# A row softmax on one core: load 5 in two transfers of 14 and 2 rows, and store 0 issued after the 14 rows

## The chip, the core and the metric

The kernel runs on one core of a Trainium2 chip. The core has five engines with instruction streams of their own: TensorE (PE, not used here), VectorE (DVE), ScalarE (ACT), GpSimd (POOL) and SyncE (SP), which here issues all transfers. Sixteen DMA engines move data between the chip's memory (HBM) and the core's on-chip memory (SBUF, 128 partitions). The metric is device time in microseconds (us) of one execution; lower is better.

## The reference

A softmax over the last axis of a float32 array of 16 x 1024 x 512, that is, over 16,384 rows of 512 numbers:

```python
def reference(x):
    x_max = np.max(x, axis=-1, keepdims=True)
    exp_x = np.exp(x - x_max)
    return (exp_x / np.sum(exp_x, axis=-1, keepdims=True)).astype(np.float32)
```

Each of input and output is 33.55 MB, so 67.1 MB cross between HBM and SBUF at least once.

## The kernel before

**Tiles.** The rows are cut into 8 chunks of 2,048 rows. In a chunk each of the 128 partitions holds 16 rows, which lie one behind the other in HBM: 16 x 512 x 4 bytes = 32 KB per partition, 4 MB per chunk. The buffer `held` has 6 places of one chunk. Chunks 6 and 7 use the places of chunks 0 and 1 again, once these are stored. All work is done in place: `held` is loaded, turned into exponentials, scaled and stored.

**Groups.** Work on the engines goes by groups of 8 rows per partition, two groups per chunk, 16 in all (128 x 4,096 numbers each). For each group:

- DVE takes the negated maximum of each row (`rowmax`, L133);
- ACT takes exp(x - max) row by row, with the row's sum as a by-product (`exps`, L165, 8 instructions per group);
- DVE takes the reciprocal of the sums (L142);
- POOL multiplies the rows by it (`scale`, L144). For groups 12 to 15 DVE does this itself (`ON_VECTOR`).

DVE's order is written out: the maximum of group g, then the reciprocal (and for the last four, the product) of group g - 1.

**Transfers.** All 16 transfers go through one DMA queue that SP feeds. `ORDER` sets the order in which SP issues them: loads 0 to 5, stores 0, 1 and 2, loads 6 and 7, stores 3 to 7. Loads 0 to 5 are issued at once, the first ahead of the kernel's opening barrier (`loads_at_the_head`, with `AT_HEAD`). A store waits until both groups of its chunk are scaled (semaphore `scaled[k]`). Load 6 waits until store 0 has landed (`stored[0]`), load 7 until store 1 has. DVE's first maximum in a chunk waits until its load has landed (`loaded[k]`). SP works through its list in order: what stands behind a waiting instruction waits too. A transfer of one chunk is 128 pieces of 32 KB, 8 for each of the 16 DMA engines. At the end SP waits until the last stores have landed.

Of the kernel before, what the change touches and what calls it, by code (L numbers as in the profile page):

```python
# [1 line left out]

# [4 lines left out]

F32 = mybir.dt.float32
EXP = mybir.ActivationFunctionType.Exp
AX = mybir.AxisListType.X  # L10

CHUNK = 16
CHUNKS = 8
PLACES = 6
GROUP = 8
PER = CHUNK // GROUP
GROUPS = CHUNKS * PER
RING = PLACES * PER  # L20


ORDER = [("L", k) for k in range(PLACES)] + [
    ("S", 0),
    ("S", 1),
    ("S", 2),
    ("L", 6),
    ("L", 7),
    ("S", 3),
    ("S", 4),  # L30
    ("S", 5),
    ("S", 6),
    ("S", 7),
]


ON_VECTOR = (12, 13, 14, 15)


AT_HEAD = {mybir.EngineType.SP: 1}  # L40

def loads_at_the_head(nc):

    main, body = nc.main_func.blocks[0], nc.main_func.blocks[1]
    for engine, count in AT_HEAD.items():
        loads = [
            i
            for i in body.instructions  # L50
            if i.engine == engine and type(i).__name__ == "InstDMACopy"
        ][:count]
        barrier = next(
            n
            for n, i in enumerate(main.instructions)
            if i.engine == engine and type(i).__name__ == "InstDrain"
        )
        for load in loads:
            body.instructions.remove(load)
        main.instructions[barrier:barrier] = loads  # L60


@with_exitstack
def kernel(
    ctx: ExitStack,
    tc: tile.TileContext,
    x: bass.AP,
    out: bass.AP,
):
    nc = tc.nc  # L70
    nc.at_finalize(loads_at_the_head)
    P = nc.NUM_PARTITIONS

    x_rows = x.flatten_outer_dims().rearrange("(c p r) d -> c p r d", p=P, r=CHUNK)
    out_rows = out.flatten_outer_dims().rearrange("(c p r) d -> c p r d", p=P, r=CHUNK)
    n, _, _, d = x_rows.shape
    assert n == CHUNKS

    held = nc.alloc_sbuf_tensor("held", [P, PLACES * CHUNK, d], F32).ap()
    shift = nc.alloc_sbuf_tensor("shift", [P, GROUPS * GROUP], F32).ap()  # L80
    sums = nc.alloc_sbuf_tensor("sums", [P, GROUPS * GROUP], F32).ap()
    recip = nc.alloc_sbuf_tensor("recip", [P, GROUPS * GROUP], F32).ap()

    loaded = [nc.alloc_semaphore(f"loaded{k}") for k in range(CHUNKS)]
    stored = [nc.alloc_semaphore(f"stored{k}") for k in range(CHUNKS)]
    maxed = nc.alloc_semaphore("maxed")
    expd = nc.alloc_semaphore("expd")
    to_pool = nc.alloc_semaphore("to_pool")
    to_vector = nc.alloc_semaphore("to_vector")
    scaled = [nc.alloc_semaphore(f"scaled{k}") for k in range(CHUNKS)]  # L90

    def take(engine, semaphore, n):

        engine.wait_ge(semaphore, n).then_inc(semaphore, -n)  # L94

    def place(k):
        at = (k % PLACES) * CHUNK
        return held[:, at : at + CHUNK, :]

    def rows(g):  # L100
        at = (g % RING) * GROUP
        return held[:, at : at + GROUP, :]

    def stats(t, g):
        return t[:, g * GROUP : (g + 1) * GROUP]

    with tc.manual_schedule():  # L110
        for _, k in ORDER[:PLACES]:
            first = nc.sync.dma_start(out=place(k), in_=x_rows[k])
            first.then_inc(loaded[k], 16)
            tc.no_tile_sem_insts.add(first.ins.name)
    tc.close()
    tc.compile()  # L116

    reused = set()
    for what, k in ORDER[PLACES:]:
        if what == "L":  # L120
            if k >= PLACES:
                take(nc.sync, stored[k - PLACES], 16)
                reused.add(k - PLACES)
            nc.sync.dma_start(out=place(k), in_=x_rows[k]).then_inc(loaded[k], 16)
        else:
            take(nc.sync, scaled[k], PER)
            nc.sync.dma_start(out=out_rows[k], in_=place(k)).then_inc(stored[k], 16)


    def rowmax(g):  # L130
        if g % PER == 0:
            take(nc.vector, loaded[g // PER], 16)
        nc.vector.reduce_max(  # L133
            out=stats(shift, g), in_=rows(g), axis=AX, negate=True
        ).then_inc(maxed, 1)

    def scale(g):
        engine, ready = (
            (nc.vector, to_vector) if g in ON_VECTOR else (nc.gpsimd, to_pool)
        )  # L140
        take(nc.vector, expd, 1)
        nc.vector.reciprocal(out=stats(recip, g), in_=stats(sums, g)).then_inc(ready, 1)  # L142
        take(engine, ready, 1)
        engine.tensor_mul(  # L144
            out=rows(g),
            in0=rows(g),
            in1=stats(recip, g).unsqueeze(2).to_broadcast([P, GROUP, d]),
        ).then_inc(scaled[g // PER], 1)

    for g in range(GROUPS):  # L150
        rowmax(g)
        if g:
            scale(g - 1)
    scale(GROUPS - 1)


    nc.scalar.preload_act_table(EXP)  # L157

    def exps(first, turns):
        with nc.scalar.Fori(0, turns) as i:  # L160
            take(nc.scalar, maxed, 1)
            for r in range(GROUP):
                row = held[:, bass.ds(i * GROUP + r, 1), :]
                at = bass.ds(i * GROUP + (first * GROUP + r), 1)
                act = nc.scalar.activation(  # L165
                    out=row,
                    in_=row,
                    func=EXP,
                    bias=shift[:, at],
                    scale=1.0,  # L170
                    accum_out=sums[:, at],
                )
            act.then_inc(expd, 1)

    exps(0, RING)
    exps(RING, GROUPS - RING)


    for k in range(CHUNKS):
        if k not in reused:  # L180
            take(nc.sync, stored[k], 16)


# [1 line left out]
_INS = ['x']  # L185
_OUTS = [((16, 1024, 512), 'float32')]


# [23 lines left out]
```

## Time and profile before

| What | Value |
|---|---|
| Median of three runs | 160.18 us (160.12 to 160.20) |
| The profiled execution's own time | 160.32 us |
| Its span, first to last instruction | 159.0 us |
| HBM read and written | 33.55 and 33.55 MB, 422 GB/s over the span |
| Maxima on DVE (L133), 16 | 70.3 us busy, 4.398 us each |
| Exponentials on ACT (L165), 128 | 90.3 us busy, 0.706 us each |
| Products on POOL (L144), 12 | 83.8 us busy, 7.018 us each |
| Products on DVE (L144), 4 | 18.3 us busy, 4.576 us each |
| Issue of loads 0 to 5 by SP | from 0.00 to 3.23 us |
| Issue of stores 0, 1, 2 by SP | at 37.65, 51.60 and 65.55 us |
| Issue of loads 6, 7 by SP | at 71.28 and 81.05 us |
| Issue of the last store by SP | at 141.02 us |

The profile is of one execution with the hardware profiler on, which is why its own time stands beside the median. The span leaves out what lies before the first and after the last instruction. Busy times are per engine and overlap. A DMA issue on SP is short; the transfer itself goes on in the DMA engines, and "landing" is the moment at which its semaphore has counted all 16 engines. The profile also holds packet records: start, duration and size of each piece that a DMA engine moved.

### The profile page before, as it was taken

To read this page: it belongs to the slowest core of one execution; us is meant where nothing else is said; L and a number is where in the kernel's file an instruction comes from. 1 tells how busy PE (TensorE), PEld (TensorE's weight loads), DVE (VectorE), ACT (ScalarE), POOL (GpSimd) and SP (SyncE) were. 2 spreads that over 40 slices of the span, in tenths; PEclk is the share of its full clock that TensorE was granted. 3 is DMA by queue.
4 is the path that set the end of the run, shared out by engine and by line. 5 is a ranking of instruction groups with operands and counts; after the bars stand their busy time and mean duration, and the time that the engine had idled before them with its cause. 6 is when DMAs were issued, how large, how long until landed. Compare 5 with 4: busy or idle time off the path is not lost. (4 is left out here: it accounts for less than half of the span.)

```text
span 159.0 us, 740 instructions
## 1 busy us (share of the span) xinstructions
DVE 90.6 (57%) x36; ACT 92.0 (58%) x257; POOL 84.0 (53%) x16
## 2 busy tenths in 40 slices
DVE  0008959777977977887700000695999998740000
ACT  0300699999999999999993000059934929200000
POOL 0000009999999999999999999259200000000000
DMA  7999999999999999999999999999999999999995
GB/s 264 470 445 404 404 478 437 396 470 445 404 404 470 445 396 396 396 412 470 437 396 445 470 404 404 478 437 398 437 437 437 412 462 414 437 437 429 429 429 256
DMA packets 2306, 67.13 MB, mean 422 GB/s; under 512 B 256, under 2 KB 256, under 8 KB 256
## 3 DMA queue, kind: packets, MB, share of 16 engines
q1 hardware_dynamic: 2304, 67.11, 98.8%
q14 instruction: 2, 0.02, 0.0%
HBM read 33.55 MB, written 33.55 MB: 422 GB/s over the span
## 5 line engine op out<-in xcount | busy, mean ns | idle before, releaser
L165 ACT ACTIVATE held<-held,shift x128 | 90.3, 706 | 40.0 <-ACTq L94 40.0
L144 POOL TENSOR_TENSOR held<-held,recip 128x4096 f32<-128x4096 f32 x12 | 83.8, 7018 | 28.1 <-POOLq L94 28.1
L133 DVE TENSOR_REDUCE shift<-held 128x8 f32<-128x4096 f32 x16 | 70.3, 4398 | 33.3 <-DVEq L94 33.3
L165 ACT ACTIVATION_READ_ACCUMULATOR held<-held,shift x128 | 23.8, 186 | 0.0
L144 DVE TENSOR_TENSOR held<-held,recip 128x4096 f32<-128x4096 f32 x4 | 18.3, 4576 | 0.6
L142 DVE RECIPROCAL recip<-sums 128x8 f32<-128x8 f32 x16 | 3.2, 201 | 16.4 <-DVEq L94 16.4
L157 ACT ACT_TABLE_LOAD x1 | 1.3, 1283 | 4.0 <-PEq L116 4.0
L196 POOL MEMSET const-float32-0.0<- 128x1 f32 x1 | 0.1, 99 | 0.2 <-issue 0.2
L196 POOL MEMSET const-uint8-127<- 128x1 uint8 x1 | 0.1, 103 | 0.0
L196 POOL MEMSET const-bfloat16-1.0<- 128x1 bf16 x1 | 0.1, 102 | 0.0
L196 POOL MEMSET const-float32-1.0<- 128x1 f32 x1 | 0.1, 99 | 0.0
## 6 DMA issues: line engine op xcount, KB each, us to landing
held<-in_x_dram SPq DMA_DIRECT2D x8, 4096.0 KB, 29.9
out_dram<-held SPq DMA_DIRECT2D x8, 4096.0 KB, 28.3
```

Of the source, the lines that this page charges most:

```text
L133: nc.vector.reduce_max(out=stats(shift, g), in_=rows(g), axis=AX, negate=True).then_inc(maxed, 1)
L142: nc.vector.reciprocal(out=stats(recip, g), in_=stats(sums, g)).then_inc(ready, 1)
L144: engine.tensor_mul(out=rows(g), in0=rows(g), in1=stats(recip, g).unsqueeze(2).to_broadcast([P, GROUP, d]),).then_inc(scaled[g // PER], 1)
L157: nc.scalar.preload_act_table(EXP)
L165: act = nc.scalar.activation(out=row, in_=row, func=EXP, bias=shift[:, at], scale=1.0, accum_out=sums[:, at],)
L196: nc = _bacc.Bacc("TRN2", target_bir_lowering=False, num_devices=1)
```

## The change

Load 5 (rows 80 to 95 of each partition) becomes two transfers: rows 80 to 93 (28 KB per partition) and rows 94 and 95 (4 KB per partition). Both are issued at the head with the other loads. Behind them SP's list has a new entry "W": SP waits until the 14 rows have landed, then raises a new semaphore, `passed`, and only then comes to store 0. DVE's first maximum that needs these rows waits for `passed`, and for the landing of the 2 rows too. (SP's wait leaves `loaded` of the 14 rows as it is; it is taken back at the end.)

The diff also rewrites how chunks and DVE's order are written down: chunks are named by their first and last row, and DVE's order is a list (`M` maximum, `P` product on POOL, `V` product on DVE). The order of DVE, ACT and POOL that comes out is the same as before, as are all other transfers and the place of each in HBM and SBUF.

```diff
-ORDER = [("L", k) for k in range(PLACES)] + [
-    ("S", 0),
-    ("S", 1),
-    ("S", 2),
-    ("L", 6),
...
+BLOCKS = [(0, 16), (16, 32), (32, 48), (48, 64), (64, 80), (80, 96), (96, 112), (112, 128)]
+ORDER = [
+    ("L", (0, 16)),
...
+    ("L", (64, 80)),
+    ("L", (80, 94)),
+    ("L", (94, 96)),
+    ("W", (80, 94)),
+    ("S", (0, 16)),
+    ("S", (16, 32)),
+    ("S", (32, 48)),
+    ("L", (96, 112)),
+    ("L", (112, 128)),
+    ("S", (48, 64)),
...
+    ("S", (112, 128)),
 ]
+AHEAD = 7
...
+    def in_dram(rows, a, b):
+
+        first, last = next(k for k in BLOCKS if k[0] <= a and b <= k[1])
+        block = rows[first * P : last * P].rearrange("(p r) d -> p r d", p=P)
+        return block[:, a - first : b - first, :]
...
+    def load(k):
+        copy = nc.sync.dma_start(out=rows(*k), in_=in_dram(x_rows, *k))
+        copy.then_inc(loaded[k], 16)
+        return copy
...
+    for what, k in ORDER[AHEAD:]:
+        if what == "W":
+
+            nc.sync.wait_ge(loaded[k], 16).then_inc(passed, 1)
+        elif what == "L":
+            for s in stores:
+                if meets(s, k[0] - RING, k[1] - RING) and s not in taken:
+                    take(nc.sync, stored[s], 16)
+                    taken.add(s)
+            load(k)
         else:
-            take(nc.sync, scaled[k], PER)
-            nc.sync.dma_start(out=out_rows[k], in_=place(k)).then_inc(stored[k], 16)
...
     def rowmax(g):
-        if g % PER == 0:
-            take(nc.vector, loaded[g // PER], 16)
+        for k in loads:
+            if meets(k, *group(g)) and k not in seen:
+                if ("W", k) in ORDER:
+                    take(nc.vector, passed, 1)
+                else:
+                    take(nc.vector, loaded[k], 16)
+                seen.add(k)
...
+    for what, k in ORDER:
+        if what == "W":
+            take(nc.sync, loaded[k], 16)
```

## The prediction, made before the changed kernel was run

> **What bounds the kernel now.** I read the page first: the busy shares, the 40 slices, the DMA part and the chain that ended last.
>
> ```profile
> span 159.0 us, 740 instructions
> DVE 90.6 (57%) x36; ACT 92.0 (58%) x257; POOL 84.0 (53%) x16
> DMA  7999999999999999999999999999999999999995
> q1 hardware_dynamic: 2304, 67.11, 98.8%
> DVE held L144 3%
> ```
>
> No compute engine is busy for even 60% of the span, while the 16 DMA engines work in every slice and the one queue fills 98.8% of their time. The chain is nearly empty (3%): the last instruction waited for a transfer, and a transfer is no step of the chain. So the bound is the queue of sixteen 4 MB transfers, and a change is worth only what it does to a hole in that queue. To find holes I cut the span at the landings of successive transfers (issue start plus time to landing) and asked for the work in each stretch. The columns are start:end and length in us, the busy time of DVE, ACT and POOL with counts, the clock, the DMA share and GB/s.
>
> ```profile
> 0.00:12.34 12.34, 0.00 (x0) 1.28 (x1) 0.21 (x4) 1.00 0.93 382
> 12.34:22.03 9.69, 8.74 (x2) 4.82 (x13) 0.00 (x0) 1.00 1.00 433
> 41.45:51.16 9.71, 7.62 (x3) 9.71 (x29) 9.71 (x2) 1.00 1.00 432
> 51.16:61.44 10.28, 8.97 (x4) 10.28 (x30) 10.28 (x3) 1.00 1.03 408
> 61.44:71.20 9.76, 7.52 (x5) 9.76 (x29) 9.76 (x2) 1.00 1.00 430
> 80.97:90.78 9.81, 0.00 (x0) 4.06 (x12) 9.81 (x2) 1.00 0.99 428
> 90.78:100.47 9.69, 0.00 (x0) 0.00 (x0) 9.54 (x2) 1.00 1.00 433
> 100.47:110.33 9.86, 8.81 (x3) 5.00 (x15) 5.02 (x1) 1.00 1.02 435
> 110.33:120.08 9.75, 8.70 (x3) 6.40 (x19) 2.00 (x1) 1.00 1.02 438
> ```
>
> These are loads 0, 1, 4, 5, store 0, store 2, loads 6 and 7, and store 3. The usual transfer takes 9.7 us. Two do not: load 0, which starts from an empty queue, and load 5, the last before the first store, which takes 10.28, so 10.28 - 9.71 = 0.57 us too long. The second change from loads to stores (load 7, then store 3) costs only 0.15, and that from store 2 to load 6 nothing.
>
> Then I looked closely at load 5's end. Each DMA engine moves one partition's 32 KB in 1.21 us, and the 16 start together, so a fine cut shows bursts of starts and pauses (GB/s is credited to a packet's start).
>
> ```profile
> 57.35:58.05 0.70, 0.70 (x1) 0.70 (x4) 0.70 (x1) 1.00 1.80 749
> 58.05:58.65 0.60, 0.60 (x1) 0.60 (x3) 0.60 (x2) 1.00 0.00 0
> 58.65:59.25 0.60, 0.60 (x1) 0.60 (x3) 0.60 (x1) 1.00 3.31 874
> 59.25:60.55 1.30, 1.30 (x1) 1.30 (x5) 1.30 (x1) 1.00 0.00 0
> 60.55:61.20 0.65, 0.65 (x1) 0.65 (x3) 0.65 (x1) 1.00 1.88 807
> 61.20:61.75 0.55, 0.32 (x1) 0.55 (x3) 0.55 (x1) 1.00 0.00 0
> 61.75:62.40 0.65, 0.00 (x0) 0.65 (x4) 0.65 (x1) 1.00 1.87 807
> ```
>
> Load 5's last packets start by 59.25 and the engines take up nothing new until 60.55: a pause of 1.30 where the others last 0.55 to 0.60. In the packet records these packets last 1.69 to 2.19 us, 1.98 in the mean, so 0.77 over 1.21. Store 0's own packets are again all 1.21. The whole question is what this stretch is: the price of having stores queued behind a load, or the price of the first store of a run.
>
> **The change, part by part.** *The split.* The same bytes go in two transfers. Packets of 28 KB and 4 KB stand in no record of before; in proportion to bytes the 2 rows last 9.71 x 2/16 = 1.21 us. The records of 4 bytes that signal a landing take 0.009 us each, so eight packets per engine with some 0.01 us of fixed time would add 0.08. Below nothing it can't go, since the bytes are the same; I take 1.21. The extra issue on SP (0.33 to 0.53 us, by the six at the head) lies under load 0, which lands at 12.34.
>
> *The wait.* Without the stretch load 5 would land at 51.16 + 9.71 = 60.87, and the 14 rows 1.21 earlier, at 59.66. SP needs 0.08 from a landing to the next issue (store 0 landed at 71.20, load 6 was issued at 71.28). So store 0 is issued at 59.74, not at 37.65. Queued behind it on SP is store 1 (ready at 51.60, now issued about 0.35 us after store 0; its packets are due some 10 us later) and store 2 (ready at 65.55, unmoved); so nobody else waits for SP. VectorE's first maximum over load 5 waits for a signal that SP gives at 59.7, and for the 2 rows at about 60.9. It runs at 68.39 today, so 7.5 us cover that.
>
> *From issue to first byte.* What counts is whether the queue runs dry. Its last packets of the 2 rows end where load 5 would have ended without stretch, at 59.80 to 60.45. The only issue into an empty queue in this trace is the first load, at 0.00 (the first line cuts the first 4 us into tenths of a us and gives the DMA share; the others are stretches as above):
>
> ```profile
> DMA  0000000000999090099900000000799799070000
> 0.00:1.00 1.00, 0.00 (x0) 0.00 (x0) 0.21 (x4) 1.00 0.00 0
> 2.00:2.80 0.80, 0.00 (x0) 0.00 (x0) 0.00 (x0) 1.00 0.00 0
> 2.80:3.60 0.80, 0.00 (x0) 0.00 (x0) 0.00 (x0) 1.00 1.55 655
> ```
>
> Its first packets start between 1.02 and 1.93, and the second round, which shows that the first is through, starts between 2.85 and 3.52. Put at store 0: first packets at 60.76 to 61.67, second round at 59.74 + 2.85 = 62.59 to 59.74 + 3.52 = 63.26. Today the second round starts at 61.80 to 62.36. The difference is +0.79 at the front and +0.90 at the back; I take +0.85.
>
> The bounds: if the store's descriptors reach the engines at once and the stretch goes with its cause, the 0.57 is won (-0.57). If every engine gets its packets as late as the last did at the head (1.93) and the store then pays a fresh 0.77 on 1.21, the second round starts at 59.74 + 1.93 + 1.98 = 63.65 at worst, 1.29 behind 62.36. I take +0.85 because load 0 is the nearest row (same queue, same size, empty) and includes a first-packet stretch like the one seen at load 5.
>
> The Trainium skill, "DMA: Bandwidth & Descriptors", section "Latency and other measured facts", gives about 0.6 us to the first byte for a transfer issued from SP. This trace shows 1.02 for the earliest engine. By the page's figure the store would be there at an estimated 59.74 + 0.6 = 60.34, before the slowest engine is through at 60.45, and the sum would be that of rival 2.
>
> *What is late next.* Loads 6 and 7 wait for stores 0 and 1 and come 0.85 later; the maximum of group 12 moves from 100.60 to 101.45, the last scaling's end from 140.92 to 141.8. Store 7 is issued then, and its place in the queue comes up at about 149 when store 6 lands (149.29 today), so 7 us cover it and the tail is unchanged.
>
> **Sum.** Split 0, wait and refill +0.85 on the DMA queue, everything behind moved by the same. Profiled time 160.32, of which the span is 159.0; the median of the runs is 160.18, 0.14 less. 160.18 + 0.85 = 161.0.
>
> **Rivals.**
>
> 1. *Order is all that counts: no change.* Store 0's packets come behind load 5's anyway, and the refill costs about what the stretch cost. First packets at 60.76 to 61.67 without a stretch of their own, against 60.59 to 61.15 today: between -0.39 (all at the early end, against today's last) and +0.52, so 159.8 to 160.7, middle 160.2. For it: store 0, issued at 37.65, took 33.5 us to land and came 9.76 behind load 5, so it waited its turn. The Trainium skill says in the same page, section "Queues, rings and completion order", that each engine consumes descriptors in ring order; the trace agrees, by that 33.5 us. Against it: the first packets of load 0 were not 1.21 but 1.41 to 2.37 us.
>
> 2. *Faster.* Place: load 5's last packets. The stretch of 0.57 is caused by a store waiting behind them in the queue, and with the store held back it is gone; the 2 rows (1.21 us) bridge the refill. It decides if the first packets come within 60.45 - 59.74 = 0.71 us of the issue and last 1.21. Time 160.18 - 0.57 = 159.6. For it: the hole is where loads and queued stores meet. Against it: load 7 also has a store queued behind it (store 3, issued at 81.5) and loses 0.15; and the one refill seen took 1.02.
>
> 3. *Worse than the sum.* The 1.29 of the upper bound, or small packets at a 32 KB pitch that run slower than by bytes, with the 14 rows landing late as well: 161.5 to 162.
>
> **How the numbers follow.** I see the first-store reading as likelier, since the stretch appears once per direction (first load, first store) and nearly vanishes at the second change from loads to stores. Forecast 0.50 (160.6 to 161.5, centre 161.0); rival 1 0.20; rival 2 0.23; rival 3 0.07. A measurement here tells 0.2%, 0.32 us, from no change. Faster: rival 2 and 0.03 of rival 1, 0.26. Same: 0.14 of rival 1 and 0.01 of the forecast, 0.15. Slower: the rest, 0.49 + 0.03 + 0.07 = 0.59. The range from rival 2's 159.6 to 161.6 takes in both bounds of the refill; outside lie half of rival 2's spread and most of rival 3. The likeliest case alone is 160.6 to 161.5.
>
> **What would show it.** In the profile after: store 0 issued near 59.7 (if not, the change doesn't do what it says); the pause before its first packets, 1.30 now, longer; its first packets longer than 1.21; store 0 landing near 72.05 against 71.20; all later transfers at 9.7 again. Rival 1 shows first packets near 60.8 to 61.2 that last 1.21. I am wrong if store 0 lands at or before 71.2: then the stretch belongs to the queued store, or the refill is under 0.7 us.

## The result, and the profile after

| | before | after |
|---|---|---|
| Median, four runs each on one chip | 160.19 us (160.12 to 160.69) | 161.89 us (161.71 to 161.95) |
| Ratio after / before | | 1.0103, 95% interval 1.0085 to 1.0121 |
| The profiled execution, and its span | 160.32 and 159.0 us | 161.71 and 160.4 us |

The change costs 1.7 us, twice the 0.85 that was forecast, and 161.89 lies above the upper end of the range. The page of the changed kernel hardly shows it:

```profile
span 160.4 us, 744 instructions
DVE 90.7 (57%) x36; ACT 92.0 (57%) x257; POOL 84.0 (52%) x16
DMA  7999999999998989999999999999999999999996
q1 hardware_dynamic: 2448, 67.11, 98.7%
```

The engines do what they did, the queue is as full as before (98.7% against 98.8%), the bytes are the same. So packets lasted longer, or a little time lay between them. The stretches from landing to landing of the changed kernel, with the columns of the prediction, say where:

```profile
51.17:60.94 9.77, 8.48 (x4) 9.77 (x29) 9.77 (x3) 1.00 1.02 433
60.94:70.99 10.05, 7.82 (x5) 10.05 (x30) 10.05 (x2) 1.00 0.97 417
70.99:80.83 9.84, 6.57 (x4) 9.84 (x29) 9.84 (x3) 1.00 0.99 426
80.83:91.41 10.58, 0.00 (x0) 4.18 (x12) 10.58 (x2) 1.00 1.00 396
91.41:101.13 9.72, 0.00 (x0) 0.00 (x0) 8.91 (x2) 1.00 1.00 432
101.13:112.12 10.99, 9.02 (x4) 6.13 (x17) 6.14 (x1) 1.00 1.01 400
112.12:121.53 9.41, 9.30 (x3) 5.26 (x16) 0.87 (x1) 1.00 0.98 425
```

These are load 5 (both parts), stores 0, 1 and 2, loads 6 and 7, and store 3. Load 5 is no longer too long, and store 0 lands at 70.99, 0.21 *earlier* than before (71.20). The time is lost later, in two transfers that the diff doesn't touch: store 2 (10.58 against 9.81) and load 7 (10.99 against 9.86, of which store 3 gives 0.34 back). Against before, landing by landing: store 0 -0.21, store 1 +0.07, store 2 +0.77, load 6 +0.03, load 7 +1.13, store 3 -0.34, stores 4 to 7 together -0.06. The sum is +1.39, the difference of the two last landings (160.35 and 158.96) and of the two profiled executions. The medians differ by 1.70; the profiled execution of the changed kernel lies 0.18 below its median and that of before 0.13 above, which is the rest.

Both places are changes of direction: store 2 is the last store before load 6, load 7 the last load before store 3. A fine cut of the changed kernel around store 0 and around those two:

```profile
60.40:60.65 0.25, 0.25 (x1) 0.25 (x1) 0.25 (x1) 1.00 0.00 0
60.65:60.85 0.20, 0.20 (x1) 0.20 (x2) 0.20 (x1) 1.00 6.19 2621
60.85:61.90 1.05, 0.66 (x1) 1.05 (x5) 1.05 (x1) 1.00 0.00 0
61.90:62.08 0.18, 0.00 (x0) 0.18 (x1) 0.18 (x1) 1.00 6.90 2913
88.70:88.90 0.20, 0.00 (x0) 0.00 (x0) 0.20 (x1) 1.00 9.65 2621
88.90:90.40 1.50, 0.00 (x0) 0.00 (x0) 1.50 (x1) 1.00 0.00 0
109.65:110.80 1.15, 0.43 (x1) 1.15 (x3) 1.15 (x1) 1.00 0.00 0
```

All 16 engines start store 0 within 60.65 to 60.85, and the second round follows after 1.24 us: no stretch. The last packets of store 2 start within 0.20 of each other (88.70 to 88.90), and then nothing is taken up for 1.50 us where 1.05 would do. At load 7 the pause is 1.15 where 0.55 to 0.60 was usual before. So the stretch that before stood at the end of load 5 is gone from there and stands twice further on.

From here on a change of direction is called a turn: load 5 to store 0, store 2 to load 6, load 7 to store 3. For the experiments one number per turn is handy: the time by which packets exceed 1.213 us per 32 KB, summed around the turn in the packet records and divided by 16 engines. Before: 0.82 at load 5's end, nothing at store 2, 0.09 at load 7. After: 0.16, 0.85 and 0.87.

### The profile page after: what moved, and what is told of

It is laid out like the page before. It is cut to its first block, busy times and chain, and to the rows that moved or that the text cites. A ratio compares the mean times of both kernels' runs of the same rounds, so it can differ in the third digit from the quotient of the medians.

```text
span 160.4 us, 744 instructions
## 1 busy us (share of the span) xinstructions
DVE 90.7 (57%) x36; ACT 92.0 (57%) x257; POOL 84.0 (52%) x16
## 3 DMA queue, kind: packets, MB, share of 16 engines
q1 hardware_dynamic: 2448, 67.11, 98.7%
```

## The experiments

Three theories stood first. "In step": the refill at store 0 puts the 16 engines in step (their starts lie 0.15 apart, 0.5 to 0.65 before), and engines that turn together are stretched. (At load 7 of the changed kernel the starts lie 0.64 apart again, and it is stretched all the same; so this theory could at best explain store 2.) "Held store": issuing store 0 late is itself the cause. "Pieces": the smaller packets or the extra landing signal are.

**Split only.** The line `("W", (80, 94))` is taken out of `ORDER`; store 0 is queued early.

> Load 5 in 14 and 2 rows, but SP doesn't wait: store 0 is queued behind both at 37.65 us. Theory 'in step' (a change of direction costs 0.6 to 0.8 us when the 16 DMA engines reach it within some 0.5 us of one another, and next to nothing when they are spread wider; the refill in the changed kernel put them within 0.15): the queue never runs dry, so all stays as before: 160.2, a stretch of about 0.6 at the end of load 5, store 2 at 9.8 and load 7 at 9.9. Rival 'pieces' (the 28 KB and 4 KB packets or the extra landing signal disturb what follows): 161.9, with store 2 near 10.6 and load 7 near 11.0 as in the changed kernel.

Measured: 160.28, ratio 1.0006 (0.9997 to 1.0016). The lines are load 5 with both parts, store 2 and load 7:

```profile
51.12:61.39 10.27, 8.93 (x4) 10.27 (x30) 10.27 (x3) 1.00 1.04 415
80.93:90.73 9.80, 0.00 (x0) 4.08 (x12) 9.80 (x2) 1.00 0.99 428
100.44:110.16 9.72, 8.81 (x3) 4.87 (x13) 4.88 (x1) 1.00 1.00 432
```

The stretch is where it was before, the other turns are clean. "Pieces" falls: the split alone costs nothing that can be measured, and the stretches come with the wait.

**Wait only.** Load 5 in one transfer, SP waits for all of it.

```diff
-    ("L", (80, 94)),
-    ("L", (94, 96)),
-    ("W", (80, 94)),
+    ("L", (80, 96)),
+    ("W", (80, 96)),
...
-AHEAD = 7
+AHEAD = 6
```

(`AHEAD` is the number of loads issued at the head.)

> Load 5 in one transfer, and SP waits until all of it has landed before store 0. Load 5 unstretched lands near 60.9, store 0 is issued near 60.95, and its first packets start 0.85 to 1.0 later, in step, 1.1 us later than in the changed kernel. Theory 'in step': store 2 and load 7 are stretched as in the changed kernel: 161.9 + 1.1 = 163.0. Rival 'pieces': no stretch at store 2 and load 7, so 163.0 - 1.5 = 161.5. Rival 'held store' (a store issued late costs later, however the gap is bridged): 163.0.

Measured: 163.17, ratio 1.0185 (1.0168 to 1.0202). Store 0, store 2 and load 7:

```profile
61.03:72.32 11.29, 9.04 (x5) 11.29 (x34) 11.29 (x2) 1.00 0.98 418
82.17:92.78 10.61, 0.00 (x0) 3.02 (x10) 10.61 (x2) 1.00 1.01 395
102.50:112.98 10.48, 8.81 (x3) 5.61 (x16) 5.63 (x1) 1.00 1.00 400
```

The open gap shows in store 0 (11.29), and the two later stretches come without any split. The 2 rows thus did what they are for, some 1.3 us against this run.

**A longer bridge.** Load 5 in 12 and 4 rows (`(80, 92)`, `(92, 96)`, W on the 12).

> Load 5 in 12 and 4 rows, store 0 issued when the 12 have landed (near 58.5 us): 2.4 us of loads are left, more than the 0.85 to 1.0 from issue to first packet, so the queue doesn't run dry and the engines keep their spread of 0.5 to 0.6. Theory 'in step': the stretch at the end of load 5 is back (about 0.6), store 2 and load 7 take 9.8 and 9.9: 160.2. Rival 'held store': no stretch at load 5, but store 2 and load 7 stretched: 161.9. Rival 'pieces': 161.9.

Measured: 160.76, ratio 1.0037 (1.0023 to 1.0052), between the forecasts. Store 0, store 2 and load 7:

```profile
60.80:70.61 9.81, 7.58 (x5) 9.81 (x30) 9.81 (x2) 1.00 0.99 428
80.48:90.21 9.73, 0.00 (x0) 4.40 (x14) 9.73 (x2) 1.00 1.03 428
99.90:110.78 10.88, 8.94 (x4) 6.02 (x17) 6.30 (x2) 1.00 0.99 389
```

Store 0 is issued at 58.48 and the queue never runs dry; the engines start its first packets up to 0.6 apart, as spread as before. Yet load 5 is not stretched (store 0 lands at 70.61, 0.59 early) and load 7 is (1.01 per engine; store 2 only 0.35, with nothing on the last engine). So "in step" is wrong about load 5 and load 7: load 7's last packets start 0.82 apart and are stretched more than any turn so far.

**Engines pushed apart, twice.** In the changed kernel the last 4 rows of store 1 are cut by partitions, so that 8 engines get more work:

```diff
+        return [(0, P, a, b - n), (0, 112, b - n, b), (112, 120, b - n, b), (120, P, b - n, b)]
...
```

> The changed kernel with the last 4 rows of store 1 cut by partitions (112, 8 and 8), so that 8 of the 16 engines move 16 KB more than the others there: they fall about 0.6 us behind, on purpose. The heavier engines end about 0.3 us later than with an even split. Theory 'in step': the stretches at store 2 and load 7 (0.7 and 0.8 a packet) vanish or shrink strongly: 161.9 - 1.5 + 0.3 = 160.7. Rivals 'held store' and 'pieces': both stretches stay: 162.2.

Measured: 165.32, far off both. The pieces themselves cost 3.3 us: store 1 lands at 84.14, against 80.83, with 32 KB packets of up to 2.1 us right after them. That drowns what was to be seen; this run decides nothing. The second try leaves the stores whole and adds a copy in HBM (chunk 7's rows are written once more, later, by store 7):

```diff
+    ("N", (112, 120)),
     ("S", (32, 48)),
...
+            nc.sync.dma_start(
+                out=in_dram(out_rows, *k)[0:8], in_=in_dram(x_rows, *k)[0:8]
+            ).then_inc(nudged, 16)
```

> The changed kernel with one more transfer between stores 1 and 2: 8 pieces of 16 KB from input to output in HBM (rows of chunk 7, which store 7 writes again later), so 8 of the 16 engines fall 0.6 us behind the others. Theory 'in step': store 2 and load 7 lose their stretches: 161.9 - 1.5 + 0.6 = 161.0. Rival 'held store': the stretches stay: 162.5.

Measured: 162.29, ratio 1.0139 (1.0123 to 1.0154). The packet records show eight engines about half a packet behind from 81 us on (at store 2 the starts lie 1.2 us apart), and the stretches are still there: 0.63 at store 2, 0.67 at load 7. Spread alone doesn't cure them.

**A dry queue without a held store.** Loads 1 to 5 wait until load 0 has landed; load 5 is whole and store 0 is queued early.

```diff
     ("L", (0, 16)),
+    ("W", (0, 16)),
...
-AHEAD = 7
+AHEAD = 1
```

> Loads 1 to 5 wait until load 0 has landed, so the queue runs dry once at 12 us (1.4 to 1.5 us lost there) and all engines start load 1 in step; load 5 is whole and store 0 is queued early as before. Theory 'in step': load 5's end is stretched by 0.6 to 0.9 as before and store 2 and load 7 are stretched too: 160.2 + 1.45 + 1.5 = 163.1. Rival 'held store' (only holding store 0 back brings the later stretches): 160.2 + 1.45 = 161.6, with store 2 and load 7 at 9.8 and 9.9.

Measured: 162.79, ratio 1.0167 (1.0151 to 1.0182). Load 1, load 5, store 2 with load 6, load 7 with store 3:

```profile
12.21:24.41 12.20, 8.95 (x3) 7.30 (x21) 0.94 (x1) 1.00 0.95 387
53.55:63.90 10.35, 8.11 (x5) 10.35 (x31) 10.35 (x2) 1.00 1.01 405
83.31:102.76 19.45, 0.00 (x0) 2.50 (x8) 16.92 (x3) 1.00 1.00 431
102.76:122.46 19.70, 17.61 (x6) 11.40 (x32) 7.02 (x1) 1.00 0.99 428
```

The gap is larger than thought (load 1 takes 12.20, 2.5 over, not 1.45), and it makes up nearly all of the 2.67 over before. Load 5 has its usual stretch, and the turns after it are clean, as their pairs are about as long as before (19.45 against 19.50, 19.70 against 19.61). So a queue that runs dry ahead of load 5's turn leaves the later turns free. A test of "in step" it isn't: the engines did not start together. Load 1 was issued at 12.30, and its first 16 packets start between 13.28 and 14.00:

```profile
12.30:13.28 0.98, 0.90 (x1) 0.00 (x0) 0.00 (x0) 1.00 0.00 0
13.28:14.00 0.72, 0.72 (x1) 0.00 (x0) 0.00 (x0) 1.00 2.54 728
```

At store 2 they are 0.45 apart, much as before (0.59). What speaks against "in step" are the stretched turns with engines far apart: load 7 of the changed kernel (0.64 apart), of the bridge of 4 rows (0.82), and both turns of the run with the copy (1.1 to 1.2). For the size at store 2 the spread may still matter: of the runs that pay there, in the table further on and in the one with the copy, those with starts within 0.2 pay 0.85 to 0.92, those with wider ones 0.35 to 0.76.

**Both load-to-store turns filled late.** As the bridge of 4 rows, and load 7 likewise in 12 and 4 rows, store 3 waiting for the 12.

> As the run with 12 and 4 rows of load 5, and load 7 too in 12 and 4 rows, with store 3 issued only when the 12 rows have landed. Theory 'queued turn' (a change of direction is stretched when the transfers of the other direction are already queued behind it, unless the engines are in a favourable spread; issued 1 to 2 us ahead of the turn it is not stretched): neither load 5 nor load 7 is stretched, 160.18 - 0.57 = 159.6, and store 0 lands near 70.6. Rival 'in step' (the spread of the engines alone decides at load 7): load 7 takes 10.9 again, 160.8.

Measured: 159.91, ratio 0.9988 (0.9979 to 0.9997). Store 0, store 2, load 7 with both parts:

```profile
60.88:70.59 9.71, 7.49 (x5) 9.71 (x28) 9.71 (x2) 1.00 1.00 432
80.32:90.18 9.86, 0.00 (x0) 4.61 (x14) 9.86 (x2) 1.00 1.03 425
100.10:109.88 9.78, 8.81 (x3) 4.92 (x14) 5.08 (x2) 1.00 1.03 441
```

Neither load is stretched: a store issued about 2 us ahead of its turn avoids the stretch *at that turn*. It is the only version whose time and profile both come out below before, by 0.12% in time; that it didn't reach 159.6 lies at store 2 and load 6 (0.49 per engine; load 6 takes 9.92) and at store 4, which takes 10.02.

**All three.** Store 2 too in 12 and 4 rows, load 6 waiting for the 12 (a new entry "X": SP waits until that store has landed).

> As the run before it, and store 2 too in 12 and 4 rows, with load 6 issued only when the 12 rows have landed, so that all three changes of direction meet a queue that is filled late. Theory 'queued turn': the mean stretch of 0.35 per engine at the end of store 2 goes as well; as the slowest engine had none there, 159.6 to 159.4. Rival 'in step': load 7 is stretched all the same, 160.8; if the late issue of load 6 lets the queue run dry, up to 1 us more.

Measured: 160.29, ratio 1.0011 (1.0002 to 1.0020), 0.7 to 0.9 above the forecast. Store 2 with both parts, and load 6:

```profile
80.24:90.01 9.77, 0.00 (x0) 4.68 (x14) 9.77 (x2) 1.00 1.06 440
90.01:100.50 10.49, 0.00 (x0) 0.00 (x0) 10.20 (x2) 1.00 0.98 408
```

At this turn from stores to loads the late issue doesn't help: load 6's first packets are stretched instead (0.62 per engine).

**More turns.** The pattern so far: the first load-to-store turn that meets a queued store is stretched, and only that one; holding a store passes it on to the next. To test it, store 3 is moved between loads 6 and 7, which makes a third such turn; once with store 0 early and load 5 whole, once held with the bridge of 4 rows.

```diff
     ("L", (96, 112)),
-    ("L", (112, 128)),
     ("S", (48, 64)),
+    ("L", (112, 128)),
```

> The kernel before with store 3 moved between loads 6 and 7, so there are five changes of direction (load 5 to store 0, store 2 to load 6, load 6 to store 3, store 3 to load 7, load 7 to store 4), all with the next transfers queued early. Theory 'first queued turn' (of the load-to-store turns that meet an already queued store only the first of the run is stretched, by 0.6 to 1.1 us; holding a store back moves that to the next such turn): load 5 takes 10.3, loads 6 and 7 9.7 to 9.9: 160.2. Rival 'spread' (each turn is stretched or not by how the engines happen to stand): loads 6 or 7 may take 10.5 or more, 160.2 to 162.

> The same five turns with load 5 in 12 and 4 rows and store 0 held until the 12 have landed. Theory 'first queued turn': no stretch at load 5, load 6 takes 10.7 to 10.9 (the first queued load-to-store turn), load 7 9.7 to 9.9: 160.7. Rival 'after a hold every later turn is stretched': loads 6 and 7 both near 10.8: 161.8.

Measured: 160.26, ratio 1.0020 (0.9994 to 1.0045; single runs from 160.05 to 161.75), and 160.85, ratio 1.0062 (1.0032 to 1.0092; from 160.55 to 162.37). With store 0 early, load 5, load 6 and load 7:

```profile
51.05:61.32 10.27, 8.95 (x4) 10.27 (x30) 10.27 (x3) 1.00 1.01 408
90.64:100.16 9.52, 0.00 (x0) 0.00 (x0) 9.52 (x2) 1.00 1.02 441
110.08:119.75 9.67, 5.24 (x2) 6.34 (x18) 1.94 (x1) 1.00 1.01 435
```

With store 0 held, the same three:

```profile
51.19:60.97 9.78, 8.51 (x4) 9.78 (x29) 9.78 (x3) 1.00 1.01 432
90.29:100.97 10.68, 0.00 (x0) 0.00 (x0) 10.01 (x2) 1.00 1.01 393
111.18:120.74 9.56, 5.24 (x2) 6.05 (x18) 1.65 (x1) 1.00 1.00 432
```

In the profiled executions it is as forecast: early, load 5 pays (0.69) and loads 6 and 7 don't; held, load 5 doesn't, load 6 pays 1.07, load 7 is clean. But two of the ten early runs and four of the ten held ones took 161.3 us or more, the held ones near what the rival gives (161.8). The profiled executions, 160.05 and 160.79, are not among them, so what those lost isn't known.

**How late is late.** Load 5 in 8 and 8 rows, store 0 issued after the first 8.

> Load 5 in 8 and 8 rows, store 0 issued when the first 8 have landed, near 56.0 us, with 4.85 us of loads left instead of 2.4. If the stretch comes whenever the store stands in the queue some us before the turn: load 5's second part is stretched by 0.6 and load 7 is clean, 160.2. If any store not queued from the first loads on counts as held: no stretch there, load 7 takes 10.9, 160.8 as with 4 rows.

Measured: 160.06, ratio 0.9987 (0.9975 to 0.9999). Load 5 with both parts, store 2, load 7:

```profile
51.15:61.37 10.22, 8.93 (x4) 10.22 (x29) 10.22 (x3) 1.00 1.03 414
80.87:90.63 9.76, 0.00 (x0) 4.12 (x12) 9.76 (x2) 1.00 0.99 426
100.66:110.66 10.00, 8.81 (x3) 5.14 (x15) 5.16 (x1) 1.00 1.00 430
```

Store 0, issued at 56.20, is some 5 us ahead of the turn: load 5 is stretched again (0.65), the later turns are clean (under 0.1). It counts as early. With 2 us (the bridge of 4 rows) it counts as late.

**Load 7 of the changed kernel treated alike** (14 and 2 rows, store 3 waits for the 14).

> The changed kernel with load 7 treated like load 5 (14 and 2 rows, store 3 issued when the 14 have landed). Theory 'queued turn': load 7's stretch (10.99 against 9.86) is gone, that at store 2 (10.58) stays: 161.9 - 1.1 = 160.8, less up to 0.3 more if the queue runs dry there. Rival 'the refill at store 0 alone sets both later stretches': 161.9.

Measured: 161.96, ratio 1.0110 (1.0081 to 1.0140). Store 2, load 7 with both parts, store 3 and store 4:

```profile
80.64:91.25 10.61, 0.00 (x0) 4.22 (x12) 10.61 (x2) 1.00 1.00 395
101.00:111.28 10.28, 8.81 (x3) 5.42 (x15) 5.43 (x1) 1.00 0.97 415
111.28:120.86 9.58, 8.95 (x3) 5.99 (x18) 1.58 (x1) 1.00 1.02 438
120.86:131.54 10.68, 10.39 (x6) 6.51 (x19) 0.00 (x0) 1.00 1.03 440
```

The profile agrees with the theory (0.11 at load 7, 0.85 at store 2), the time does not; it is the rival's 161.9, and by luck, as the rival has load 7 stretched: what load 7 gains is lost again, at the refill (load 7 still takes 10.28) and at store 4, where one engine alone falls about 1 us behind with two packets of 1.5 us. Why that engine does is open.

**After the first turn has paid.** Is it the first such turn of the run, or does every late fill bring the stretch back? Store 1 waits until store 0 has landed (the queue runs dry), or until its first 12 rows have (it doesn't); store 0 is early in both. The diff is that of the second.

```diff
-    ("S", (0, 16)),
+    ("S", (0, 12)),
+    ("S", (12, 16)),
+    ("X", (0, 12)),
     ("S", (16, 32)),
...
```

> The kernel before with store 1 issued only when store 0 has landed: load 5's turn meets a queued store and is stretched as before (10.3), and the queue runs dry once after that, near 71 us, which costs about 1.3 us (landing to next landing as at store 0 of the run that held load 5 whole: 11.29 against 9.76, less what the start in step takes back). Theory 'first queued turn of the run': the turn at load 5 has paid, load 7 stays at 9.7 to 9.9: 160.2 + 1.5 = 161.7. Rival 'dry queue' (a queue that ran dry brings the stretch back at the turns after it): store 2 near 10.6 and load 7 near 11.0, 163.3.

> As the run before it, but store 0 goes in 12 and 4 rows and store 1 is issued when the 12 have landed, so the queue is filled late and doesn't run dry. Theory 'first queued turn of the run': as before, 160.2. Rival 'late fill' (any transfer that reaches the engines late, within 2.4 us of its turn, brings the stretch back at the next turns, without a dry queue): load 7 near 10.9, 161.2.

Measured: 163.71, ratio 1.0209 (1.0153 to 1.0265), and 162.36, ratio 1.0107 (1.0042 to 1.0173; single runs from 161.44 to 162.69). Run dry, load 5, store 1, store 2 and load 7:

```profile
51.10:61.37 10.27, 9.01 (x4) 10.27 (x29) 10.27 (x3) 1.00 1.01 408
71.09:82.40 11.31, 6.29 (x4) 11.31 (x33) 11.31 (x3) 1.00 0.98 417
82.40:93.10 10.70, 0.00 (x0) 2.51 (x8) 10.70 (x2) 1.00 0.99 392
102.82:113.91 11.09, 9.02 (x4) 6.22 (x17) 6.24 (x1) 1.00 1.00 400
```

Filled late but not dry, store 1, store 2, load 6 and load 7:

```profile
71.13:80.81 9.68, 6.25 (x4) 9.68 (x29) 9.68 (x3) 1.00 1.01 433
80.81:91.00 10.19, 0.00 (x0) 4.09 (x12) 10.19 (x2) 1.00 1.00 408
91.00:102.11 11.11, 0.00 (x0) 0.00 (x0) 9.19 (x2) 1.00 0.99 419
102.11:112.74 10.63, 8.81 (x3) 5.76 (x17) 5.79 (x1) 1.00 0.99 398
```

"First turn of the run" falls. Load 5 pays, and after the late fill store 2 and load 7 pay too: 0.89 and 0.83 dry, 0.76 and 0.75 bridged. No hole is to be seen where the bridged fill happens (store 1 takes 9.68). The time of the bridged run misses its rival's 161.2 by 1.2 us all the same: store 2 and load 6 together take 21.30 against 19.50 before, 1.8 more, with single packets of up to 2.67 us, while the mean over the engines is 0.76. Why the engines share the cost so unevenly in that run isn't shown.

The time over 1.213 us per 32 KB at each turn, in us per engine, over all runs that can be compared (a dash: under 0.06; the load 5 column includes store 0's first rounds). A "late fill" is a transfer issued 2 us or less before the engines come to it, or after they have run out of work. Small packets of a split count for up to 0.08 of these numbers. Each row is one profiled execution:

| Run | late fill at | load 5 to store 0 | store 2 to load 6 | next load to store | the one after |
|---|---|---|---|---|---|
| before | none | 0.82 | - | 0.09 | |
| split only | none | 0.83 | - | - | |
| loads 1 to 5 wait | load 1 | 0.78 | - | - | |
| five turns | none | 0.69 | - | - | - |
| bridge of 8 rows | none (5 us ahead) | 0.65 | 0.06 | 0.08 | |
| **the change** | store 0 | 0.16 | 0.85 | 0.87 | |
| wait only | store 0 | 0.06 | 0.92 | 0.75 | |
| bridge of 4 rows | store 0 | 0.09 | 0.35 | 1.01 | |
| five turns, held | store 0 | 0.09 | 0.35 | 1.07 | - |
| stores 0 and 3 held | stores 0, 3 | 0.09 | 0.49 | - | |
| all three | 0, load 6, 3 | 0.09 | 0.62 | - | |
| change, load 7 too | stores 0, 3 | 0.15 | 0.85 | 0.11 | |
| dry after store 0 | store 1 | 0.65 | 0.89 | 0.83 | |
| store 1 late | store 1 | 0.76 | 0.76 | 0.75 | |

One rule fits every row: after the start of the run or a late fill, each turn costs 0.35 to 1.1 us until a load-to-store turn has met stores that were queued early; that turn pays too, and from then on turns are free (under 0.1). A store-to-load turn pays without ending it. One kind of turn is excepted: a load-to-store turn at which the stores themselves are the late fill is nearly free (0.16 at most, load 5 in seven rows and load 7 in three). The rule got this form after the runs; its part on late fills had stood in the expectations of the last two, as the rival, and was confirmed by them. It is a description. What in the DMA engines keeps that state isn't shown.

## Why the prediction was wrong

**The bound** was right: the DMA queue, 98.8% before and 98.7% after, and no engine's wait came into it. Store 7 was issued at 141.68 and store 6 landed at 150.71, so the cover of DVE's chain held.

**The split at nothing** was right: 1.0006 (0.9997 to 1.0016) by itself.

**The wait**: the 14 rows landed at 59.68 (59.66 forecast), store 0 was issued at 59.84 (59.74). SP needed 0.16, not 0.08; it has two waits to pass there, "W" and that for store 0's scaling, but that this is the reason isn't shown.

**The refill, +0.85, failed**, sign included: store 0 landed 0.21 earlier. Load 5 landed 0.50 earlier (60.94 against 61.44), as its stretch was gone, and store 0 with its refill took 0.29 more (10.05 against 9.76). I had priced the refill by the first load, as "the nearest row". Load 0's packets started 1.02 to 1.93 after the issue and lasted 1.41 to 2.37 us; store 0's started 0.85 to 1.00 after it, on all engines within 0.15, and lasted 1.24 us. The Trainium skill, "DMA: Bandwidth & Descriptors", section "Latency and other measured facts", gives about 0.6 us to the first byte; counted from the end of the issue instruction (0.35 us long) this run has 0.50 to 0.65. So load 0 was the wrong row. That it is the first transfer of the run isn't what sets it apart: in the run whose loads 1 to 5 wait, load 1 was issued into an empty queue at 12.30, and its first packets started 0.98 to 1.69 us later and lasted 1.45 to 2.15 us, much as load 0's. Stores issued into an empty queue (store 0 with the wait only, store 1 run dry) started 0.84 to 1.00 us after the issue and lasted 1.24. A store's refill was priced by a load's. Why the two differ isn't shown.

**The reading behind it failed too**: "the price of the first store of a run". Store 0 is the first store in the changed kernel as well, and the last packets ahead of it aren't stretched. The stretch does go when the store is held back, as rival 2 had it; its objection, that load 7 had a queued store and lost only 0.15, falls with the rule above: load 5 had paid before.

**"Everything behind moved by the same", all later transfers at 9.7**, is the step that put the time out of the range. Store 2 and load 7 lost 0.77 and 1.13, 1.9 us together, which no part of the sum and none of the rivals contained. (The measured 161.89 lies in rival 3's 161.5 to 162, but by luck: the refill was not dearer than the sum had it, and the 14 rows did not land late.) I had looked at the first turn alone and taken the other two as given, though the page of before showed them to be free right after one that was not. That the change came out slower was thus forecast for a reason that the runs refute.

**Rival 1's ring order** holds as far as it goes: the transfers landed in the order of their issue in every run. It says nothing of the packets' durations, and these moved.

## What to carry to other kernels

When a queue is the bound, a change at one place in it has to be priced at every later turn, not only where it is made: here the visible cost at load 5 went away and came back twice. On the evidence of this case, keep a bound DMA queue filled several us ahead through all changes of direction (5 us was enough in one run, about 2 us was not in any run with a bridge of 4 rows, though holding the stores back at both turns came out no slower than before, 159.91); a bridge that hides the gap hides only the gap. And price a refill by a row of its own direction: a load's row was too dear for a store here. And before a stretch is removed, ask what follows it at no cost: a cost that is seen once may be what makes the rest free.

## What the runs showed of the hardware

- A queue that is always filled well ahead paid once for its first change from loads to stores (0.65 to 0.83 us per engine in four runs, and 0.78 in one whose queue ran dry only before that) and next to nothing for those after it (under 0.1). Late fills brought the cost back, in the bridged runs without a visible hole: 0.35 to 0.92 at the next change from stores to loads, 0.75 to 1.07 at the next from loads to early stores.
- After a refill with the engines in step, packets of 32 KB lasted a little longer: 1.24 us in store 0's first two rounds in the changed kernel and about 1.22 in the later ones, against 1.213 before. This is a small part of the loss: stores 0 and 1 together still landed 0.14 us earlier.
- Going from load 0 to loads 1 to 5 through an empty queue cost 2.5 us, going from load 5 to store 0 in that way (wait only) 1.6 (11.29 against 9.7). From issue to first packet it was 0.98 to 1.69 us for load 1, and 0.85 to 1.00 for store 0 (wait only, and the changed kernel).
- The last 1 MB of store 1, cut into short transfers over 112, 8 and 8 partitions (8 KB per partition), landed 3.3 us later than whole.
